# Casting later attention weights in two pairs of quarters and merging the scan's loads, in a one-core hybrid decoder layer

## The chip, the cores and the metric

The kernel runs on one core of a Trainium2 chip. A core has TensorE (PE: matrix products into PSUM), VectorE (DVE), ScalarE (ACT), GpSimd (POOL) and SyncE (SP), which here issues nearly all DMA transfers, from one queue, in order. Each engine works through its own instructions in order and waits where an instruction's operands or buffers are not ready. The metric is the device time of one execution in microseconds (us), lower is better; the time given for a kernel is a median of runs.

## The reference, cut to what matters

One layer with 1024 tokens and a model width of 1024, all in float32. Two groups of heads read the same normalised input.

```
proj = rms_norm(x, norm1_w) @ w_in          # q, k, v of attention; q, k, v, gate of DeltaNet
# group A: differential attention, 4 heads, two 64-wide softmax maps each
a    = softmax(q1 k1^T) - lam * softmax(q2 k2^T)      # causal
da_o = rms_norm(a @ v) * (1 - lam_init)
# group B: gated DeltaNet, 4 heads, in chunks, a scan that carries a state
v_new = u_c - w_c @ state
o     = (q_c * exp(g)) @ state + qk_c @ v_new
state = state * exp(g_last) + k_dec^T @ v_new
# both, then the MLP
x = x + concat(da_o, dn_o) @ w_out
x = x + relu(rms_norm(x, norm2_w) @ w_up)**2 @ w_down
```

## The kernel before

Every float32 product that must be exact is split: an operand is rounded to a short part (`wH`, `hH`: a cast on ACT) and a rest (`wL`, `hL`: a subtraction on DVE), and TensorE makes three products instead of one. So each piece of a weight passes through a DMA load into a raw buffer `wraw`, a cast on ACT (L200) and a subtraction on DVE (L201). There are two `wraw` buffers in the stage of interest, so a third load has to wait for the first buffer's cast and subtraction.

The stages follow each other roughly so: input norm and gates, DeltaNet projections (up to about 241 us of the profiled execution), then a long interleaved stage, then the MLP. In the interleaved stage run, side by side, as generators:

- `da_units`: the attention projections. There are six units, in the order k, q, v of heads 0 and 1, then k, q, v of heads 2 and 3. A unit has 256 columns of `w_in` (four quarters of 256 KB, each two of the eight k-blocks) and eight blocks of 128 rows; a block makes 24 products of 128x256 (L941 to L943). Behind each block ACT copies the result out of PSUM (L952 or L959 and L960). Blocks of q and k are normalised and turned: `da_turns` transposes them (L906, L907), ACT and DVE make `qa`, and SP stores it to `qk_d` (L912).
- `scan` and `scan_out`: the recurrence over eight chunks of 128 tokens. `load` (L788) brings four heads of `pka`, 192 KB each; the products at L796, L808 and L819 and their readers follow each other. `scan_out` loads `pkb` (L838, 128 KB a head, five buffers) and `zgt`, multiplies at L848 and L855 and stores `mixn_d`.
- `scores` and `values`: the attention itself by query tiles: loads of `qa` and `qb` (L1003, L1004), score products at L1061, L1062 and L1064, exponentials on ACT (L1070), transposes of the probabilities (L1097), their copy `at` on ACT (L1099), value products (L1109), and the copy `om` (L1114). Transposes and value products share two PSUM banks, `px0` and `px1`; a bank is free again once ACT, or ACT and DVE, have read it.
- `mix_loads`, `mixed` and `outproj`: the output projection, which has its weights from `load_unit` too. Its first half is called `pre` and is requested in the first block of the last unit.

Two things set the order of instructions. TensorE's order is written out by a planner, the class `Interleave`: each generator yields the time from which it may go on, `flow.chain` books estimated durations on ACT ("S"), DVE ("V") and POOL ("G"), and the ready generator with the lowest priority number is taken. `unit_time` books one unit's casts and subtractions and gives the due times `wt` of the four quarters. The order on ACT, DVE, POOL and SP is made by the framework's scheduler, which plays the instructions through with its own estimates; `tc.issue_after(x)` keeps an instruction from standing ahead of `x`.

In `load_unit` a quarter is loaded, cast and subtracted in one turn of a loop, and `da_units` calls it for unit i + 1 in the first block of unit i:

```
for k in range(0, nk, st):
    ...
    nc.sync.dma_start(raw[:, :, o:o + n], src[:, k0 + k:k0 + k + st, c0:c0 + n])
    ...
    S.copy(wh[:, k:k + st, :], raw)
    eng.tensor_tensor(wl[:, k:k + st, :], raw, wh[:, k:k + st, :].bitcast(F32), ALU.subtract)
```

Of the kernel before, what the change touches and what calls it, by code (L numbers as in the profile page):

```python
# [9 lines left out]
F32 = mybir.dt.float32  # L10
# [8 lines left out]
P = 128  # L19
SEQ = 1024  # L20
DM = 1024
KB = DM // P
NT = SEQ // P
HEADS = 4
# [97 lines left out]
def tile_hymba_layer(  # L122
# [6 lines left out]
    nc = tc.nc  # L129
    V, S, G, T = nc.vector, nc.scalar, nc.gpsimd, nc.tensor  # L130
# [3 lines left out]
    w_in_v = w_in[0].rearrange("(kb p) c -> p kb c", p=P)  # L134
# [48 lines left out]
    hH = hpool.tile([P, KB, SEQ], F32R, name="hH")  # L183
    hL = hpool.tile([P, KB, SEQ], F32R, name="hL")

    def load_unit(src, ranges, k0=0, nk=KB, eng=None, rp=None):
        eng = eng or V
        width = sum(n for _, n in ranges)
        wh, wl = staged("wH"), staged("wL")
        wh = wh[:, :nk * width].rearrange("p (k c) -> p k c", k=nk)  # L190
        wl = wl[:, :nk * width].rearrange("p (k c) -> p k c", k=nk)
        st = 2 * UC // width
        for k in range(0, nk, st):
            raw = rp.tile([P, 2 * UC], F32, tag="wraw", name="wraw", bufs=8) if rp else laid("wraw")
            raw = raw[:, :st * width].rearrange("p (k c) -> p k c", k=st)
            o = 0
            for c0, n in ranges:
                nc.sync.dma_start(raw[:, :, o:o + n], src[:, k0 + k:k0 + k + st, c0:c0 + n])
                o += n
            S.copy(wh[:, k:k + st, :], raw)  # L200
            eng.tensor_tensor(wl[:, k:k + st, :], raw, wh[:, k:k + st, :].bitcast(F32), ALU.subtract)  # L201
        return wh, wl

    def mm3(ps, lh, ll, rh, rl, n):
# [143 lines left out]
    with tc.manual_schedule(engines={T.engine, V.engine, S.engine}):  # L348
# [59 lines left out]
        for tb in range(2, NT):  # L408
            ps = z_mm(tb, 0)
# [11 lines left out]
            ps = z_mm(tb, 1)  # L421
# [351 lines left out]
    def unit_time(eng="V", rate=610.0):  # L773
        done = []
        for i in range(4):
            start = flow.now if i < 2 else done[i - 2]
            done.append(flow.chain(("S", 520.0), (eng, rate), start=start + DMA_T))
        return done

    def scan():  # L780
        St = {}
        psA = pA.tile([P, 512], F32, name="ps_A")
        PA = {h: psA[:, h * P:(h + 1) * P] for h in range(HEADS)}

        def load(c):
            pka = sb.tile([P, HEADS, 3, P], F32, tag="pka", name="pka", bufs=2)
            for h in range(HEADS):
                nc.sync.dma_start(pka[:, h], park_d[h, c, :, 0:3, :])  # L788
            return pka

        nxt = load(0)
        for c in range(NT):
            pk, rr_, yy = nxt, {}, {}
            if c > 0:
                for h in range(HEADS):
                    T.matmul(PA[h], pk[:, h, 0, :], St[h], start=True, stop=True)  # L796
                for h in range(HEADS):
                    i = cidx(h, c)
                    rr_[h] = sb.tile([P, P], F32, tag="sr", name="sr", bufs=4)
                    V.scalar_tensor_tensor(rr_[h], PA[h], neg_eg[:, i:i + 1], pk[:, h, 2, :], ALU.mult, ALU.add)  # L800
                flow.pe(4 * MM)
                yield flow.chain(*[vec(P, 60)] * 4), None
            else:
                for h in range(HEADS):
                    rr_[h] = pk[:, h, 2, :]
            for h in range(HEADS):
                Wc = W[h, c // 4][:, (c % 4) * P:(c % 4 + 1) * P]
                T.matmul(PA[h], Wc, rr_[h], start=True, stop=True)  # L808
            y4 = sb.tile([P, 512], F32, tag="sy", name="sy", bufs=2)
            S.copy(y4, psA)  # L810
            if c + 1 < NT:
                nxt = load(c + 1)
            flow.pe(4 * MM)
            yield flow.chain(act(512)), None
            Sold = dict(St)
            for h in range(HEADS):
                yy[h] = y4[:, h * P:(h + 1) * P]
                if c < NT - 1:
                    T.matmul(PA[h], pk[:, h, 1, :], yy[h], start=True, stop=True)  # L819
            if c < NT - 1:  # L820
                for h in range(HEADS):
                    i = cidx(h, c)
                    Sn = sb.tile([P, P], F32, tag=f"S{h}", name=f"S{h}", bufs=2)
                    if c > 0:
                        V.scalar_tensor_tensor(Sn, St[h], elast[:, i:i + 1], PA[h], ALU.mult, ALU.add)
                    else:
                        V.tensor_copy(Sn, PA[h])
                    St[h] = Sn
                flow.pe(4 * MM)
            flow.add(1, scan_out(c, Sold, yy), 0, "pB")  # L830
            if c < NT - 1:
                yield flow.chain(*[vec(P, 60)] * 4), None

    def scan_out(c, Sold, yy):
        pkb = {}
        for h in range(HEADS):
            pkb[h] = sb.tile([P, 2, P], F32, tag="pkb", name="pkb", bufs=5)
            nc.sync.dma_start(pkb[h], park_d[h, c, :, 3:5, :])  # L838
        zgt = sb.tile([P, 512], F32, tag="zgt", name="zgt", bufs=1)
        nc.sync.dma_start(zgt, zg_d[c])  # L840
        oc = sb.tile([P, 512], F32, tag="oc", name="oc", bufs=2)
        so = sb.tile([P, 4], F32, tag="so", name="so", bufs=2)
        osq = sb.tile([P, P], F32, tag="osq", name="osq", bufs=1)
        yield flow.now + 2500, "pB"
        if c > 0:
            o1 = pB.tile([P, 512], F32, tag="pB", name="ps_o1")
            for h in range(HEADS):
                T.matmul(o1[:, h * P:(h + 1) * P], pkb[h][:, 0, :], Sold[h], start=True, stop=True)  # L848
            V.tensor_tensor(v4(oc), v4(o1), bc_col(eg[:, c::8]), ALU.mult)
            flow.pe(4 * MM)  # L850
            flow.hold("pB", flow.chain(vec(512)))
            yield flow.now, "pB"
        o2 = pB.tile([P, 512], F32, tag="pB", name="ps_o2")
        for h in range(HEADS):
            T.matmul(o2[:, h * P:(h + 1) * P], pkb[h][:, 1, :], yy[h], start=True, stop=True)  # L855
        if c > 0:
            V.tensor_tensor(oc, oc, o2, ALU.add)
        else:
            S.copy(oc, o2)
        for h in range(HEADS):  # L860
            i = cidx(h, c)
            S.activation(osq, oc[:, h * P:(h + 1) * P], AF.Square, scale=rq[:, i:i + 1], accum_out=so[:, h:h + 1])
        f = sb.tile([P, 4], F32, tag="of", name="of", bufs=2)
        rstd(f, so, 1.0 / P, EPS, sb, "oft", 4)
        V.tensor_tensor(f, f, rq[:, c::8], ALU.mult)
        for h in range(HEADS):
            V.scalar_tensor_tensor(oc[:, h * P:(h + 1) * P], oc[:, h * P:(h + 1) * P], f[:, h:h + 1],
                                   zgt[:, h * P:(h + 1) * P], ALU.mult, ALU.mult)
        nc.sync.dma_start(mixn_d[c], oc)
        flow.pe(4 * MM)  # L870
        t = flow.chain(vec(512))
        flow.hold("pB", t)
        flow.chain(*[act(P, True)] * 4, vec(4), powr(4), vec(4), *[vec(P, 60)] * 4, start=t)
        if c == NT - 1:
            s2ctx.close()
            spctx.close()
            mp = ctx.enter_context(tc.tile_pool(name="mp", bufs=1, **left))
            pools["mp"] = mp
            for tb in tiles:
                accs[tb] = row_tile("acc")  # L880
            pools["a2"] = bctx.enter_context(tc.tile_pool(name="a2", bufs=1, **left))
            pools["be"] = bctx.enter_context(tc.tile_pool(name="be", bufs=2, **left))
            pools["rsc"] = scctx.enter_context(tc.tile_pool(name="rsc", bufs=1, space=PSUM, **right))
            state["scan"] = True
# [34 lines left out]
    def da_units():  # L919
        todo = [(g, kind) for g in range(2) for kind in (1, 0, 2)]  # L920

        def unit_w(i):
            g, kind = todo[i]
            return load_unit(w_in_v, [(512 * kind + 256 * g, 256)]), unit_time()

        w = unit_w(0)
        freed = [0.0, 0.0]
# [1 line left out]
        for i, (g, kind) in enumerate(todo):  # L929
            (wh, wl), wt = w  # L930
            for tb in range(NT):
# [17 lines left out]
                    yield flow.now + 50, None  # L949
                qn = sd.tile([P, 256], F32, tag="qn", name="qn", bufs=4)  # L950
                if kind == 2:
                    S.copy(qn, ps[:, :256])  # L952
                    st = nc.sync.dma_start(v_d[g, tb], qn.rearrange("p (h e) -> p h e", h=2))
                    if g == 1:
                        prefetch_x(st)
# [1 line left out]
                else:  # L957
                    sq = sd.tile([P, 256], F32, tag="qsq", name="qsq", bufs=1)
                    S.activation(sq, ps[:, :256], AF.Square)  # L959
                    S.copy(qn, ps[:, :256])  # L960
                    sn = sd.tile([P, 4], F32, tag="sn", name="sn", bufs=2)
                    V.tensor_reduce(sn, sq.rearrange("p (a d) -> p a d", d=DQK), axis=AX.X, op=ALU.add)
                    rn = sd.tile([P, 4], F32, tag="rn", name="rn", bufs=2)
# [4 lines left out]
                    freed[n % 2] = flow.chain(act(256), start=t - flow.HOP)  # L968
                    t = flow.chain(vec(256), vec(4), powr(4), vec(256), start=t - flow.HOP)
                    late.append((g, kind, tb, qn, t))  # L970
                n += 1
                state["units"] = n
            if kind == 2:
# [766 lines left out]
```

## Time and profile before

| what | value |
|---|---|
| median of 3 runs | 1268.11 us (1265.73 to 1270.84) |
| profiled execution | 1264.09 us, span in the profile 1262.1 us |
| granted TensorE clock | 0.999 |
| busy TensorE | 1234.1 us |
| busy DVE, ACT, POOL | 817.8, 614.0, 111.0 us |
| DMA | 200.02 MB, mean 158 GB/s |

In the rows, "out<-in" are tile names, "x" a count. A wait row names the engine and line that waited, what released it, and the total, the number and the longest wait in us. A timeline row has the start in us from the beginning of the span, the duration, engine, line and operation, and in brackets the idle time ahead of it with what ended it. "SPq" is the queue of DMA issues on SP. Products are pipelined: their durations overlap, and the distance of two starts tells how fast they follow each other.

### The profile page before, as it was taken

Reading aid. Unit: us, or ns where it says so; the run is one execution under the profiler, and the core shown is the slowest. Engines: PE = TensorE matmul, PEld = TensorE weight load, DVE = VectorE, ACT = ScalarE, POOL = GpSimd, SP = SyncE. Lnnn points to the kernel's source line nnn. Section 1 sums busy time; section 2 is a strip of 40 time slices with the busy share of each in tenths; the row PEclk is TensorE's granted clock in tenths of the full one; section 3 lists DMA queues with packets and bytes.
Section 4 is the critical chain, followed back from the end, with each engine's and each line's share of the span. In section 5 each row is a group of like instructions: output and inputs, shape, how many; then the busy total and the mean of one; then the engine's idle time right before and its main releaser. Section 6 shows DMA issues by size and latency. Waiting matters only on the chain.

```text
span 1262.1 us, 18992 instructions
## 1 busy us (share of the span) xinstructions
PE 1234.1 (98%) x6973; PEld 1061.5 (84%) x6973; DVE 817.8 (65%) x1416; ACT 614.0 (49%) x1237; POOL 111.0 (9%) x141
## 2 busy tenths in 40 slices
PE   8999999999999999998999999999999999999998
PEld 7988888899998998887887888888887788888887
DVE  6557797557657647776589555665566865687553
ACT  4469554334446545665557444554554333333331
POOL 2211110022212300011200000000000000000000
PEclk9999999999999999999999999999999999999999
DMA  6135554368858656334246534534368755433311
GB/s 240 39 94 144 142 165 118 82 191 260 258 144 245 168 179 162 99 91 143 94 147 207 191 136 167 183 134 144 124 226 323 302 200 200 167 101 100 128 39 67
DMA packets 165814, 200.02 MB, mean 158 GB/s; under 512 B 20905, under 2 KB 126169, under 8 KB 165722
## 3 DMA queue, kind: packets, MB, share of 16 engines
q1 hardware_dynamic: 165720, 198.82, 48.8%
q8 instruction: 55, 0.90, 0.3%
q14 instruction: 37, 0.30, 0.1%
q10 hardware_dynamic: 2, 0.00, 0.0%
HBM read 132.71 MB, written 66.06 MB: 157 GB/s over the span
## 4 chain that ended last, share of the span: by engine, by line
PE 85%; DMA 8%; DVE 3%; ACT 2%; issue 1%; SPq 1%; POOLq 0%; DVEq 0%; POOL 0%; ACTq 0%
PE X L1368 4%; PE X L1367 4%; PE X L1366 4%; PE ps_qk L941 4%; PE ps_qk L942 4%; PE ps_qk L943 4%; PE X L1662 3%; PE X L1663 3%; PE X L1661 3%; PE ps_dn L206 3%; PE ps_dn L207 3%; PE ps_dn L208 3%; PE Y L1366 2%; PE Y L1367 2%; PE Y L1368 2%; PE ps_o L1109 2%
## 5 line engine op out<-in xcount | busy, mean ns | idle before, releaser
L1285 ACT CAST hH<-ur 128x1024 fp32r<-128x1024 f32 x56 | 58.6, 1050 | 175.6 <-PE Z L1662 85.2
L1286 DVE TENSOR_TENSOR hL<-ur,hH 128x1024 fp32r<-128x1024 f32 x56 | 68.3, 1222 | 82.4 <-ACT hH L1285 82.3
L941 PE MATMUL ps_qk<-wH,hH 128*128 128x256 f32 x384 | 114.8, 299 | 0.1
L942 PE MATMUL ps_qk<-wL,hH 128*128 128x256 f32 x384 | 108.5, 283 | 0.0
L943 PE MATMUL ps_qk<-wH,hL 128*128 128x256 f32 x384 | 108.4, 282 | 0.0
L1286 DVE TENSOR_TENSOR op<-raw,op 128x1024 fp32r<-128x1024 f32 x48 | 58.7, 1223 | 74.2 <-PE X L1367 39.5
L1662 PE MATMUL X<-hL,hH 128*128 128x512 f32 x224 | 87.4, 390 | 2.7 <-DVE hL L1286 2.7
L1661 PE MATMUL X<-hH 128*128 128x512 f32 x224 | 87.5, 391 | 1.4 <-DVE b L1563 1.4
L1663 PE MATMUL X<-hH,hL 128*128 128x512 f32 x224 | 87.3, 390 | 0.0
L206 PE MATMUL ps_dn<-hH,wH 128*128 128x512 f32 x192 | 76.2, 397 | 0.3 <-ACT cp L561 0.3
L208 PE MATMUL ps_dn<-hH,wL 128*128 128x512 f32 x192 | 76.0, 396 | 0.0
L207 PE MATMUL ps_dn<-hL,wH 128*128 128x512 f32 x192 | 75.7, 395 | 0.0
L941 PEld LDWEIGHTS ps_qk<-wH,hH 128*128 128x128 f32 x384 | 73.5, 191 | 0.3 <-ACT qn L960 0.2
L942 PEld LDWEIGHTS ps_qk<-wL,hH 128*128 128x128 f32 x384 | 73.5, 191 | 0.0
L943 PEld LDWEIGHTS ps_qk<-wH,hL 128*128 128x128 f32 x384 | 73.2, 191 | 0.0
L1286 DVE TENSOR_TENSOR hL<-dw,hH 128x1024 fp32r<-128x1024 f32 x56 | 68.0, 1217 | 3.2 <-ACT hH L1285 3.2
L1285 ACT CAST op<-raw 128x1024 fp32r<-128x1024 f32 x48 | 50.4, 1052 | 36.9 <-PE Y L1368 19.9
L1285 ACT CAST hH<-dw 128x1024 fp32r<-128x1024 f32 x56 | 58.5, 1047 | 14.8 <-PE Z L1663 8.1
L565 DVE SCALAR_TENSOR_TENSOR cy<-cp,pv,cy 128x512 f32<-128x512 f32 x72 | 53.6, 745 | 13.1 <-ACT cy L563 12.4
L201 DVE TENSOR_TENSOR wL<-wraw,wH 128x512 fp32r<-128x512 f32 x64 | 43.8, 697 | 27.8 <-ACT wH L200 27.5
L200 ACT CAST wH<-wraw 128x512 fp32r<-128x512 f32 x64 | 38.2, 621 | 43.2 <-DMA wraw<-in_w_in_dram 28.5
L1070 ACT ACTIVATE pexp<-ps_sc,mx 128x128 f32<-128x128 f32 (+7 forms) x64 | 47.4, 741 | 22.9 <-DVE mx L1066 22.6
(354 smaller groups left out, 3459.8 us busy)
## 6 DMA issues: line engine op xcount, KB each, us to landing
ur<-ud SPq DMA_DIRECT2D x28, 1024.0 KB, 5.1
raw<-in_w_up_dram SPq DMA_DIRECT2D x32, 512.0 KB, 3.9
dw<-in_w_down_dram SPq DMA_DIRECT2D x32, 512.0 KB, 7.3
wraw<-in_w_in_dram SPq DMA_DIRECT2D x48, 256.0 KB, 2.9
qk_d<-qa SPq DMA_DIRECT2D x32, 256.0 KB, 3.6
ud<-ua SPq DMA_DIRECT2D x16, 512.0 KB, 2.6
ud<-s SPq DMA_DIRECT2D x16, 512.0 KB, 2.7
pka<-park_d SPq DMA_DIRECT2D x32, 192.0 KB, 3.8
```

The lines of the kernel that those rows point to most:

```text
L206: T.matmul(ps, lh(k), rh(k), start=(k == 0), stop=False)
L207: T.matmul(ps, lh(k), rl(k), start=False, stop=False)
L208: T.matmul(ps, ll(k), rh(k), start=False, stop=(k == n - 1))
L941: T.matmul(ps[:, :256], hH[:, k, sl], wh[:, k, :], start=(k == 0), stop=False)
L942: T.matmul(ps[:, :256], hH[:, k, sl], wl[:, k, :], start=False, stop=False)
L943: T.matmul(ps[:, :256], hL[:, k, sl], wh[:, k, :], start=False, stop=(k == KB - 1))
L1285: S.copy(dst[0], src)
L1286: V.tensor_tensor(dst[1], src, dst[0].bitcast(F32), ALU.subtract)
L1366: T.matmul(ps, op[0][:, k, cs], h[0][:, k, :], start=start and k == 0, stop=False, skip_group_check=True)
L1661: T.matmul(bank[t], v[0][:, j, sl], v[2][:, j], start=s0, stop=False, skip_group_check=True)
L1662: T.matmul(bank[t], v[0][:, j, sl], v[3][:, j], start=False, stop=False, skip_group_check=True)
L1663: T.matmul(bank[t], v[1][:, j, sl], v[2][:, j], start=False, stop=s1, skip_group_check=True)
```

## The change

`load_unit` gets a parameter `later`. With it, the two first quarters are loaded at once and everything else becomes a list of steps: split (cast and subtract) quarter 0, load quarter 2, split 1, load 3, split 2, split 3. Units 2 to 5 use it. In the unit before, behind the copy of block 3, four of these steps are issued, and behind the copy of block 6 the last two; each cast is kept behind that copy. For the planner, due times of these units become 0, and two pairs of cast and subtraction are booked at each of the two places. Units 0 and 1 and all other callers work as before.

The scan's four loads of `pka` for a chunk become one transfer of four heads. The four loads of `pkb` become two transfers of two heads, in three buffers of double size.

```
-    def load_unit(src, ranges, k0=0, nk=KB, eng=None, rp=None):
+    def load_unit(src, ranges, k0=0, nk=KB, eng=None, rp=None, later=None):
...
-        for k in range(0, nk, st):
+
+        def load(k):
             raw = rp.tile([P, 2 * UC], F32, tag="wraw", name="wraw", bufs=8) if rp else laid("wraw")
...
-            S.copy(wh[:, k:k + st, :], raw)
+            raws.append(raw)
+
+        def split_part(k, behind=None):
+            raw = raws.pop(0)
+            with tc.issue_after(behind.ins) if behind else ExitStack():
+                S.copy(wh[:, k:k + st, :], raw)
             eng.tensor_tensor(wl[:, k:k + st, :], raw, wh[:, k:k + st, :].bitcast(F32), ALU.subtract)
+
+        raws, ks = [], list(range(0, nk, st))
+        if later is None:
+            for k in ks:
+                load(k)
+                split_part(k)
+            return wh, wl
+        load(ks[0])
+        load(ks[1])
+        for i, k in enumerate(ks):
+            later.append(lambda behind, k=k: split_part(k, behind))
+            if i < 2:
+                later.append(lambda behind, k=ks[i + 2]: load(k))
         return wh, wl
...
             pka = sb.tile([P, HEADS, 3, P], F32, tag="pka", name="pka", bufs=2)
-            for h in range(HEADS):
-                nc.sync.dma_start(pka[:, h], park_d[h, c, :, 0:3, :])
+            nc.sync.dma_start(pka, park_d[:, c, :, 0:3, :].rearrange("h p s e -> p h s e"))
...
-        for h in range(HEADS):
-            pkb[h] = sb.tile([P, 2, P], F32, tag="pkb", name="pkb", bufs=5)
-            nc.sync.dma_start(pkb[h], park_d[h, c, :, 3:5, :])
+        for h in (0, 2):
+            t = sb.tile([P, 2, 2, P], F32, tag="pkb", name="pkb", bufs=3)
+            nc.sync.dma_start(t, park_d[h:h + 2, c, :, 3:5, :].rearrange("h p s e -> p h s e"))
+            pkb[h], pkb[h + 1] = t[:, 0], t[:, 1]
...
+        steps = []
+
         def unit_w(i):
             g, kind = todo[i]
-            return load_unit(w_in_v, [(512 * kind + 256 * g, 256)]), unit_time()
+            if i < 2:
+                return load_unit(w_in_v, [(512 * kind + 256 * g, 256)]), unit_time()
+            return load_unit(w_in_v, [(512 * kind + 256 * g, 256)], later=steps), [0.0] * 4
...
-                    S.copy(qn, ps[:, :256])
+                    act_at = S.copy(qn, ps[:, :256])
...
+                if steps and tb in (3, 6):
+
+                    for _ in range(4 if tb == 3 else 2):
+                        steps.pop(0)(act_at)
+                    for _ in range(2):
+                        flow.chain(("S", 520.0), ("V", 610.0))
                 n += 1
```

More of the change, by code (lines that the diff above doesn't have):

```diff
@@ L959, in da_units @@
                     S.activation(sq, ps[:, :256], AF.Square)
-                    S.copy(qn, ps[:, :256])
+                    act_at = S.copy(qn, ps[:, :256])
                     sn = sd.tile([P, 4], F32, tag="sn", name="sn", bufs=2)
```

## The prediction

> **What bounds the kernel now.** First the page: the span, the busy time of the engines, the share of the chain of work by engine, and the transfers that the edit touches.
>
> ```profile
> span 1262.1 us, 18992 instructions
> PE 1234.1 (98%) x6973; PEld 1061.5 (84%) x6973; DVE 817.8 (65%) x1416; ACT 614.0 (49%) x1237; POOL 111.0 (9%) x141
> ...
> PE 85%; DMA 8%; DVE 3%; ACT 2%; issue 1%; SPq 1%; POOLq 0%; DVEq 0%; POOL 0%; ACTq 0%
> ...
> ur<-ud SPq DMA_DIRECT2D x28, 1024.0 KB, 5.1
> ...
> dw<-in_w_down_dram SPq DMA_DIRECT2D x32, 512.0 KB, 7.3
> wraw<-in_w_in_dram SPq DMA_DIRECT2D x48, 256.0 KB, 2.9
> ...
> pka<-park_d SPq DMA_DIRECT2D x32, 192.0 KB, 3.8
> ```
>
> In the last rows stand the count, the size and the median us from issue to landing; two more rows of the same kind, from the full list of transfers:
>
> ```profile
> qa<-qk_d SPq DMA_DIRECT2D x66, 64.0 KB, 2.4
> ...
> acc<-acc_d SPq DMA_DIRECT2D x8, 512.0 KB, 11.9
> ```
>
> TensorE is busy for 98% of the span. Its work is the same in both programs (6583 instructions of the same kinds), so the edit can only move the remaining 28 us of gaps and the small cost of changing from one group of products to another. The next view says how much of that lies where the order changes. In the changed program's order TensorE's instructions differ only from about 285 us to about 447 us of this trace; before and behind it they stand in the same order, and so do ACT's. Two stretches by engine (columns: stretch and length, PE, PEld, DVE, ACT, POOL busy, clock, DMA share, GB/s), then TensorE's waits from 275 to 447 us (total, times, longest).
>
> ```profile
> 280.00:345.00 65.00, 64.92 (x559) 64.75 (x558) 44.68 (x139) 28.12 (x87) 16.44 (x16) 1.00 0.83 258
> 368.00:447.00 79.00, 75.30 (x615) 71.72 (x614) 51.82 (x145) 47.37 (x135) 22.48 (x24) 1.00 0.76 216
> ```
>
> ```profile
> PE ps_qkt L906 <- ACT at L1099: 2.7, 1, 2.7
> PE ps_sc L1061 <- ACT pexp L1070: 0.7, 1, 0.7
> PE ps_qkt L906 <- ACT om L1114: 0.2, 1, 0.2
> ```
>
> The scan's stretch has 0.1 us of idle TensorE in 65 us. The whole region has 3.6 us of waits, and 2.7 of these are a single one. That wait is followed back through TensorE, ACT and the queue of SP:
>
> ```profile
> 400.45 0.28 PE L943 MATMUL ps_qk<-wH,hL 128*128 128x256 f32 x1
> 403.43 0.33 PE L906 MATMUL ps_qkt<-ident,qn 128*128 128x128 f32 x1 [2.70 <-ACT at L1099]
> ```
>
> ```profile
> 402.59 0.62 ACT L200 CAST wH<-wraw 128x512 fp32r<-128x512 f32 x1 [3.17 <-DMA wraw<-in_w_in_dram]
> 403.12 0.26 ACT L1099 COPY at<-ps_at 128x128 f32<-128x128 f32 x1
> ```
>
> ```profile
> 398.08 0.38 SPq L198 DMA_DIRECT2D wraw<-in_w_in_dram  x1
> 398.56 0.58 SPq L1003 DMA_DIRECT2D qa<-qk_d  x1
> ```
>
> A quarter of the next unit's weights is issued at 398.08 and lands at 402.59, 4.5 us later. ACT has already come to the cast of that quarter and stands there for 3.17 us. The copy `at` behind it keeps a PSUM bank occupied, and the transposes at L906 need that bank. This is head-of-line blocking on ACT by a load issued too late.
>
> **The change part by part.**
>
> *Quarters of units 2 to 5 (16 casts, 16 subtractions, 16 loads).* Number and size stay. Quarters 0 and 1 are now cast behind block 3's copy, quarters 2 and 3 behind block 6's. Their loads are issued several blocks earlier (a block is 24 products of about 0.12 us, 2.9 us, against a landing of 2.9 to 4.5 us), so no cast of these units should meet a missing transfer: the 2.7 us go, and the 0.2 with them. The 0.7 stands behind an exponential of the scores, which stays: 0 for it. A gain of 2.9; at most 3.6, if that goes too, and at least 2.7. Is the weight still in time? In the changed order the shortest way from the end of block 6 to the product that needs quarter 2 is 4.3 us (unit 2), and to quarter 3, 5.0 us. Against it stand the copies, casts and a subtraction:
>
> ```profile
> 439.12 0.37 ACT L960 COPY qn<-ps_qk 128x256 f32<-128x256 f32 x1
> 439.38 1.15 ACT L200 CAST wH<-wraw 128x512 fp32r<-128x512 f32 x2
> ```
>
> ```profile
> 403.24 0.69 DVE L201 TENSOR_TENSOR wL<-wraw,wH 128x512 fp32r<-128x512 f32 x1 [3.21 <-ACT wH L200]
> ```
>
> 0.37 + 1.15 + 0.69 is 2.2 us, so 2 us of cover are left. If it were gone, TensorE would wait at the start of each of four units; I take 0.
>
> *Regrouping.* The planner no longer sees due times for these weights, and TensorE's order between 285 and 447 us has 11 groups fewer (934 instead of 945 runs of one output). A change of group costs one longer step, as the starts show:
>
> ```profile
> 439.39 0.36 PE L941 MATMUL ps_qk<-wH,hH 128*128 128x256 f32 x1
> 439.59 0.28 PE L942 MATMUL ps_qk<-wL,hH 128*128 128x256 f32 x1
> 439.70 0.28 PE L943 MATMUL ps_qk<-wH,hL 128*128 128x256 f32 x1
> ```
>
> 0.20 us instead of 0.12, so 11 x 0.08 = 0.9 us less; between 0, if other groups lose it, and 0.9.
>
> *The first half of the output weights (`pre`), not edited, but moved in effect.* Now its quarters 0 and 1 were loaded long ahead, because the two raw buffers were free after unit 5's early casts: issued at 404.66, cast at 439.38 without a wait. Quarters 2 and 3 do wait.
>
> ```profile
> 404.66 0.38 SPq L198 DMA_DIRECT2D wraw<-in_w_out_dram  x1
> ```
>
> ```profile
> 440.76 0.93 SPq L198 DMA_DIRECT2D wraw<-in_w_out_dram  x2
> ```
>
> ```profile
> 441.33 0.27 ACT L1114 COPY om<-ps_o 128x128 f32<-128x128 f32 x1 [0.63 <-PE ps_o L1109]
> ...
> 444.54 0.62 ACT L200 CAST wH<-wraw 128x512 fp32r<-128x512 f32 x1 [2.12 <-DMA wraw<-in_w_out_dram]
> ```
>
> Landing took 3.8 us there (440.76 to 444.54), and TensorE did not mind. In the changed program unit 5's last two quarters leave the raw buffers only behind block 6 of unit 4, while `pre` is still cast behind block 7: one block for the load. From the end of block 6: copies and casts 0.7 + 1.15, subtraction 0.69, so the load is issued at 2.6 and lands 2.9 to 3.8 us later, at 5.5 to 6.4; the second a little later; two casts end at 6.7 to 7.7. Behind them on ACT stands `om` (0.27), which frees the bank for the second of two transposes. By the changed order TensorE comes to it at 6.3: five groups of six products (3.6), score products 0.6, value products 1.8, transposes 0.3:
>
> ```profile
> 432.89 0.31 PE L1061 MATMUL ps_sc<-KS,qa 128*128 128x128 f32 x1
> ...
> 433.48 0.36 PE L941 MATMUL ps_qk<-wH,hH 128*128 128x256 f32 x1
> ...
> 435.00 1.95 PE L1109 MATMUL ps_o<-vt,at 128*128 128x128 f32 x16
> ...
> 436.78 0.27 PE L906 MATMUL ps_qkt<-ident,qn 128*128 128x128 f32 x1
> ```
>
> So it waits 0.7 to 1.7 us there; then quarters 2 and 3 are loaded behind these subtractions, and the copy `at` behind their casts is 0 to 1.4 us late for the next value products. Together 0.7 to 3.1; with the 4.5 us landing seen at 398.08 instead, 5. I take 1.9, the middle of the nearer rows.
>
> *Scan loads.* An issue of `pka` takes SP 0.42 us (the columns of the durations are least, median, most, in ns):
>
> ```profile
> L788 SPq DMA_DIRECT2D pka<-park_d x16: 319/422/486, 290.8 to 334.4; - x16
> ```
>
> With 40 issues fewer (24 of `pka`, 16 of `pkb`) SP is left some 16 us, but no wait of TensorE in this stretch ends on SP or on these loads: 0. The merged `pka` (768 KB) lands between 3.8 (192 KB) and 5.1 us (1024 KB); the gap from its free buffer to its use stays above 10 us: 0. The merged `pkb` (256 KB, three buffers) is tighter. The scan runs faster in the new order, and for chunks 5, 6 and 7 the products that read it come 5.6, 5.6 and 5.2 us behind those that free its buffer. Issue 0.4 plus today's landing in this stretch,
>
> ```profile
> DMA to landing us min/median/max: 4.7/4.8/4.8
> ```
>
> gives 5.2 and, with semaphores, some 5.4: a delay of about 0.5 us in all. It is 0 at the 2.9 us of `wraw`, and 6.7 us at the 7.3 us of `dw` (7.7 less 5.6, 5.6 and 5.2). I take 0.5, from the row of the same transfer.
>
> [...]
>
> *Query loads.* The scores of the fourth tile come 2.9 us earlier in the new order, 5.6 us behind those of the second, which free their `qa` and `qb`. SP needs four issues of 0.58, a store of `qk_d` and a load of `x` (some 0.4 each) between, 3.1 us, and the last lands 2.4 later: 5.5, just in time. The store itself waits for a transposed block, up to one group of products and its two copies, some 1.3 us: 0 to 1.3 late, I take 0.7, the middle, as no row is nearer to one end.
>
> Sum: -2.9 - 0.9 + 1.9 + 0.5 + 0.7 = -0.7 us. The profiled execution took 1264.09 us (span 1262.1 and 2.0 around it), so 1263.4 in a like execution. The median of the runs is 4.0 us above it, 1268.11; the median after should be 1267.4.
>
> **The rivals.**
>
> 1. *The gain stands alone.* `pre` lands in time, as quarters 2 and 3 at 440.76 hurt nobody now, and `pkb` and the queries land in time: -2.9 - 0.9 is -3.8, 1264.3. For it: 0.1 us idle in the scan. Against: `pre` has one block of 2.9 us for the 3.8 us of landing.
>
> 2. *`pre` takes the place of the late quarter.* The same blocking of ACT moves from unit 4 to unit 5. At 5 us the sum is +2.4, 1270.5: slower than before, within 0.5%. It decides where `pre` costs over 2.6 us, between the landings of 2.9 (0.7) and 3.8 (3.1): from about 3.6 us on. For it: the 3.8 us of the very load. Against: the median of 2.9.
>
> 3. *Late scan loads.* If merged `pkb` lands like `dw`, 6.7 in place of 0.5 makes the sum +5.5, 1273.6; at the 11.9 of `acc<-acc_d` each chunk is 6.7 to 7.1 us late and the sum is +19, 1287. TensorE then waits at L848 for two heads that came in one transfer. It costs over 0.5% from a landing of about 7.6 us on. For it: the DMA share of 0.83. Against: `pkb` in that load takes 4.8.
>
> 4. *Nothing.* The casts are written later, yet ACT's order in the changed program could put them where a wait costs as much: 1268.1. Against: in the changed order of SP each of these loads stands whole blocks ahead of its cast.
>
> **How the numbers follow.** About 0.5%, 6.3 us, is what a measurement of this kernel can tell from no change. My case, with rival 4 next to it, 0.55; rival 1 0.2; rival 2 0.14; rival 3 0.11. Only rival 3 passes 6.3 us above, and only in 0.08; nothing in the region can give 6.3 us below (3.6 + 0.9 is all), except a shift of the gaps outside it, 24 of the 28 us: 0.04. The runs spread from 1265.73 to 1270.84, so a median carries some 2 us. Range: 1264.3 less 2 to 1270.5 plus 2.5, that is 1262.3 to 1273; it leaves out the upper part of rival 3 and the ends of the spread, some 0.15.
>
> **What would show it.** Right: no cast of units 2 to 5 idle on `wraw<-in_w_in_dram`, the 2.70 row gone, and a new wait of one to three us near unit 5's first blocks that follows casts idle on `wraw<-in_w_out_dram`. `pka` x8 and `pkb` x16 issues. Wrong: waits of TensorE on L796, L848 or their ACT and DVE partners in the scan; waits at the start of units on `wL`; or longer gaps behind 447 us, where the order is the same and only arrival times move.

## The result: slower by 0.5%, and the profile after

The changed kernel takes 1273.09 us in the median of four runs (1273.0 to 1275.41) against 1267.83 us of four runs of the kernel before (1265.73 to 1270.84). The ratio is 1.0052, with a 95% interval of 1.0036 to 1.0068: slower by 0.52%. Run again beside other kernels (e5), the ratio was 1.0047 (1.0033 to 1.0061). The forecast was 1267.4 us, 0.7 under the kernel before, with a range of 1262.3 to 1273: the measured time is 5.7 us above the forecast, and the kernel became slower where a slight gain was expected.

The page of the changed kernel: span, busy time by engine, and the share of the chain of work by engine.

```profile
span 1271.3 us, 18939 instructions
PE 1237.5 (97%) x6973; PEld 1063.4 (84%) x6973; DVE 819.2 (64%) x1416; ACT 614.7 (48%) x1237; POOL 111.4 (9%) x141
...
PE 82%; DMA 9%; DVE 4%; ACT 2%; issue 1%; SPq 1%; POOL 1%; POOLq 0%; DVEq 0%; ACTq 0%
```

TensorE's instructions are the same in number and kind (6973 in both pages; the 6583 of the prediction stands in neither), and its busy time is up by 3.4 us: at a lower granted clock the same products take longer (those of 128x512 start 0.43 us apart at a clock of 0.50, from 1004.86 us on, and 0.23 us apart at 1.00, from 998.86 us on). The span is 9.2 us longer. By the starts of products 1.3 us of this arise before 130 us, where the programs are equal (the granted clock from 68.6 to 130 us was 0.97 in this execution and 1.00 in that of before). The stretch from the first product of the fifth attention block to that of the 45th of 48 has nearly all the rest: 269.19 to 452.92 before, 270.36 to 461.04 after, 6.9 us more. TensorE's waits of the changed kernel in that stretch (total, times, longest in us):

```profile
PE ps_sc L1091 <- DMA qa<-qk_d: 3.8, 1, 3.8
PE ps_qkt L926 <- ACT om L1144: 1.4, 1, 1.4
PE ps_o L868 <- DMA pkb<-park_d: 1.0, 1, 1.0
PE ps_sc L1091 <- ACT pexp L1100: 0.6, 1, 0.6
PE ps_qkt L926 <- DVE qn L990: 0.6, 1, 0.6
PE ps_sc L1092 <- DMA qb<-qk_d: 0.4, 1, 0.4
PE ps_qkt L926 <- ACT at L1129: 0.4, 1, 0.4
```

These are 8.2 us where the kernel before had 3.6 in the same stretch (the three rows that the prediction shows). The 2.7 us behind `at` are gone. The new large one is a wait of score products for the queries, `qa` and `qb`. In TensorE's order of time it is the third tile of head 0 (384 columns):

```profile
382.27 0.41 PE L1091 MATMUL ps_sc<-KS,qa 128*128 128x384 f32 x1 [3.78 <-DMA qa<-qk_d]
383.13 0.49 PE L1092 MATMUL ps_sc<-KS,qb 128*128 128x384 f32 x1 [0.44 <-DMA qb<-qk_d]
```

SP's queue says why the queries were late (start, duration of the issue, line, transfer):

```profile
367.56 1.26 SPq L1018 DMA_DIRECT2D KS<-qk_d  x2
369.66 0.38 SPq L1025 DMA_DIRECT2D vt<-v_d  x1
370.08 2.04 SPq L1018 DMA_DIRECT2D KS<-qk_d  x2
372.16 1.20 SPq L1025 DMA_DIRECT2D vt<-v_d  x1
373.41 2.42 SPq L1184 DMA_DIRECT2D mt<-mixn_d  x2
375.93 0.58 SPq L1033 DMA_DIRECT2D qa<-qk_d  x1
```

Ahead of the third tile's queries stand four loads of head 1's keys (`KS`, 256 KB each), two of values (`vt`, 512 KB each, one of head 0 and one of head 1) and two of `mt` (256 KB each): 2.5 MB, of which only head 0's values stood there before as well. In the kernel before the same queue had these queries first and the first of head 1's keys behind them:

```profile
369.74 0.60 SPq L1003 DMA_DIRECT2D qa<-qk_d  x1
...
371.69 0.61 SPq L1004 DMA_DIRECT2D qb<-qk_d  x1
372.40 0.53 SPq L198 DMA_DIRECT2D wraw<-in_w_in_dram  x1
372.97 1.26 SPq L988 DMA_DIRECT2D KS<-qk_d  x2
```

Nothing in the diff touches these loads. They wait for the scan's memory (`KS` and `vt` of head 1 and `mt` lie in it). In TensorE's new order the scan ends some 3 us earlier (its last store is issued at 364.35 against 367.46), and in SP's order, which the scheduler writes, they now stand ahead of the queries.

The wait costs more than itself. The stretches of the changed kernel around it (stretch and length, PE, PEld, DVE, ACT, POOL busy, clock, DMA share, GB/s):

```profile
378.50:382.27 3.77, 0.00 (x0) 0.03 (x1) 0.75 (x2) 0.00 (x0) 0.00 (x0) 1.00 1.07 313
382.27:383.13 0.86, 0.41 (x2) 0.19 (x2) 0.00 (x0) 0.00 (x0) 0.00 (x0) 1.00 1.04 343
383.13:386.00 2.87, 2.87 (x12) 2.43 (x13) 1.11 (x2) 1.47 (x5) 0.00 (x0) 0.53 0.88 257
386.00:388.00 2.00, 2.00 (x17) 2.00 (x16) 1.43 (x6) 1.50 (x7) 0.00 (x0) 0.82 0.53 127
```

Behind the pause the clock is 0.53 and then 0.82: 2.87 x 0.47 + 2.00 x 0.18 is 1.7 us of lost work. In the kernel before the pause of 2.70 us (400.73 to 403.43) had no such trail; the same view there, in two stretches of 3.41 us:

```profile
398.74:402.15 3.41, 1.99 (x17) 1.79 (x16) 1.29 (x3) 0.68 (x2) 0.38 (x1) 1.00 1.00 319
402.15:405.56 3.41, 2.13 (x18) 2.13 (x19) 2.10 (x6) 2.97 (x8) 0.00 (x0) 1.00 0.65 190
```

So the stretch adds up: 8.2 - 3.6 = 4.6 us of waits and 1.7 us of clock, 6.3 of the 6.9.

### The profile page after: what moved, and what is told of

Read it like the earlier page. It is cut to its first block, busy times and chain, and to the rows that moved or that the text cites. A ratio compares the mean times of both kernels' runs of the same rounds, so it can differ in the third digit from the quotient of the medians.

```text
span 1271.3 us, 18939 instructions
## 1 busy us (share of the span) xinstructions
PE 1237.5 (97%) x6973; PEld 1063.4 (84%) x6973; DVE 819.2 (64%) x1416; ACT 614.7 (48%) x1237; POOL 111.4 (9%) x141
## 4 chain that ended last, share of the span: by engine, by line
PE 82%; DMA 9%; DVE 4%; ACT 2%; issue 1%; SPq 1%; POOL 1%; POOLq 0%; DVEq 0%; ACTq 0%
PE X L1398 4%; PE X L1396 4%; PE X L1397 4%; PE X L1692 3%; PE X L1693 3%; PE X L1691 3%; PE ps_qk L965 3%; PE ps_dn L226 3%; PE ps_dn L228 3%; PE ps_dn L227 3%; PE ps_qk L967 3%; PE ps_qk L966 3%; PE Y L1396 2%; PE Y L1397 2%; PE Y L1398 2%; PE ps_o L1139 2%
## 5 line engine op out<-in xcount | busy, mean ns | idle before, releaser
L1096 DVE TENSOR_REDUCE mx<-ps_sc 128x1 f32<-128x128 f32 (+7 forms) x64 | 47.8, 754 | 25.0 <-PE ps_sc L1094 24.5
```

## The experiments

Three theories stood against each other for the loss. Q: the order of loads in SP's queue delays the queries, and the clock falls because of that wait. M: the merged transfers of the scan are slow and disturb what follows. C: the clock falls in these executions for another reason, and the wait is a small matter. Each kernel ran beside the kernel before on the same chip, in five rounds.

**e1_scan_only.** The kernel before with only the scan's loads merged.

```
+            nc.sync.dma_start(pka, park_d[:, c, :, 0:3, :].rearrange("h p s e -> p h s e"))
...
+        for h in (0, 2):
+            t = sb.tile([P, 2, 2, P], F32, tag="pkb", name="pkb", bufs=3)
```

> The kernel before with the scan loads merged alone; TensorE's order is that of before. Theory Q (the loss comes from the queue: the planner's new order ends the scan earlier, so keys and values of head 1 and the normalised mix, 2.5 MB, stand ahead of the third tile's queries): no change, within 2 us of before; the wait of 2.7 us behind the late quarter stays. Theory M (the merged transfers hold others up): slower by 3 us or more, with waits on pkb or in the scan. Theory C (the clock is granted lower whenever this kernel family runs longer, whatever the loads do): no statement on the mean, a clock of 0.996 or less.

Measured: 1263.37 us against 1265.35, ratio 0.9987 (0.9974 to 1.0). The merged loads alone cost nothing, and the median is even 2.0 us lower; M falls. Its wait in the stretch is the old one behind `at`, but it lasts 3.4 us in this execution, and behind it the clock falls (the wait ends at 404.48):

```profile
PE ps_qkt L906 <- ACT at L1099: 3.4, 1, 3.4
```

```profile
402.00:404.00 2.00, 0.00 (x0) 0.00 (x0) 0.00 (x0) 0.36 (x1) 0.00 (x0) 1.00 1.07 300
404.00:406.00 2.00, 1.52 (x7) 1.53 (x8) 1.49 (x5) 2.00 (x6) 0.00 (x0) 0.53 0.44 145
406.00:408.00 2.00, 2.00 (x13) 2.00 (x12) 2.00 (x4) 0.85 (x3) 0.00 (x0) 0.62 0.53 176
```

The same wait, at 2.70 us in the profile of the kernel before, left the clock alone. The last section comes back to this.

**e2_weights_only.** The changed kernel with the scan's loads as before, four and four.

```
-            nc.sync.dma_start(pka, park_d[:, c, :, 0:3, :].rearrange("h p s e -> p h s e"))
+            for h in range(HEADS):
+                nc.sync.dma_start(pka[:, h], park_d[h, c, :, 0:3, :])
...
```

> The changed kernel with the scan loads as before, four and four; TensorE's, ACT's and DVE's order are those of the changed kernel. Theory Q: nearly all of the loss, 4 to 5 us slower than before; a wait of 3 to 4 us on qa at the third tile's scores, and the clock dip behind it; the wait on pkb of 1.0 us gone. Theory M: back to the time of before, since no merged transfer is left. Theory C: slower by as much as the changed kernel, with or without the wait.

Measured: 1268.59 us against 1265.35, ratio 1.0028 (1.0014 to 1.0042). The loss comes with the weights' part: 3.2 us, where 4 to 5 were expected. Whether it is smaller than in the whole change the intervals don't say. The profile has the same wait, longer than the 3 to 4 us expected, and the clock after it:

```profile
PE ps_sc L1091 <- DMA qa<-qk_d: 6.1, 1, 6.1
```

```profile
380.00:384.00 4.00, 1.56 (x4) 1.02 (x5) 0.07 (x1) 0.00 (x0) 0.00 (x0) 0.50 0.58 170
384.00:388.00 4.00, 4.00 (x19) 3.69 (x19) 2.33 (x7) 2.83 (x9) 0.00 (x0) 0.50 0.61 198
```

**e3_queries_first.** The changed kernel, with head 1's loads and the first two of `mt` kept behind the fourth tile's last query load in SP's queue. TensorE's order is that of the changed kernel.

```
-                heads[1] = load_head(1, pools["a2"]), load_v(1, pools["a2"])
+                with tc.issue_after(asked[3].ins):
+                    heads[1] = load_head(1, pools["a2"]), load_v(1, pools["a2"])
...
-            nc.sync.dma_start(mt, (mixn_d if i < NT else mixa_d)[t])
+            with tc.issue_after(asked[3].ins) if i < 2 else ExitStack():
+                nc.sync.dma_start(mt, (mixn_d if i < NT else mixa_d)[t])
```

> The changed kernel with one thing moved: the loads of head 1's keys and values and the first two loads of the mix are kept behind the fourth tile's queries in SP's queue; TensorE's order is that of the changed kernel. Theory Q: the wait of 3.8 us on qa, the 1.4 us on qb (in part) and the dip of the clock to 0.66 behind them go; 5 to 6 us less than the changed kernel, so 1267 to 1268, near before; mean clock 0.998 or more apart from an early dip. Theory M: no change against the changed kernel. Theory C: clock stays at 0.993 to 0.996 and the time within 2 us of the changed kernel.

Measured: 1261.65 us against 1265.35, ratio 0.9975 (0.9961 to 0.9989). The order of a few loads on SP turns the loss into a gain, and the mean clock of the profile is 1.000, so C falls and Q holds. The gain is larger than expected: 9.6 us less than the changed kernel in e5, on the same chip, where 5 to 6 were forecast. Of the wait on `qa` 0.7 us is left, now at the fourth tile:

```profile
PE ps_qkt L926 <- ACT om L1148: 1.4, 1, 1.4
PE ps_o L868 <- DMA pkb<-park_d: 0.7, 1, 0.7
PE ps_sc L1095 <- DMA qa<-qk_d: 0.7, 1, 0.7
```

**e4_old_plan.** The changed kernel, but the planner sees units 2 to 5 as before (due times from `unit_time`, no bookings behind blocks 3 and 6), so that TensorE's order is that of the kernel before.

```
-            return load_unit(..., later=steps), [0.0] * 4
+            return load_unit(..., later=steps), unit_time()
...
-                    for _ in range(2):
-                        flow.chain(("S", 520.0), ("V", 610.0))
```

> The changed kernel, but the planner books units 2 to 5 as before (due times and bookings in the first block), which gives TensorE the order of before; loads, casts and merged transfers stay changed. Theory Q: the third tile's queries have 0.5 MB ahead of them instead of 2.5, no wait on qa there, and the 2.7 us behind the late quarter are gone: 1 to 3 us faster than before, if the first half of the output weights costs 1 to 2 us at unit 5. Theory M: slower than before by what e1 shows. Theory C: no statement on the mean, clock 0.996 or less.

Measured: 1262.74 us against 1265.35, ratio 0.997 (0.9957 to 0.9982). With the old order of TensorE, and with it the old end of the scan, the change as a whole brings 2.6 us, as expected. How much of this the later casts bring isn't shown: the merged loads alone (e1) gave 2.0 us, and the intervals overlap. No wait for queries of more than 0.4 us is left in the stretch, and the 2.70 us are gone, but other waits have come, two of them longer than 1 us:

```profile
PE ps_o L868 <- DMA pkb<-park_d: 1.6, 1, 1.6
PE ps_qkt L926 <- DVE rnt L251: 1.1, 1, 1.1
```

In this one execution the waits sum to 4.9 us against 3.6 in the profile of before, and the stretch from the fifth to the 45th block takes 186.5 us against 183.7, with 1.7 us lost to a clock of 0.50 from 325.24 to 328.65 us.

**e5_after_again.** The changed kernel once more, as the base of the next three.

> The changed kernel once more, beside the next three on one chip. Both theories: about 1.0 to 1.005 of the kernel before, with a wait of some 4 us of the third tile's first score products on qa. If it comes out no slower than the kernel before here, the loss is one of single executions and not of the order of the loads.

Measured: 1271.27 us against 1265.13, ratio 1.0047 (1.0033 to 1.0061). The wait on `qa` was 5.0 us here, with a clock of 0.50 behind it; `pkb` was not waited for.

**e7_only_x.** The changed kernel with only the two `mt` loads behind the queries.

```
+            with tc.issue_after(asked[3].ins) if i < 2 else ExitStack():
+                nc.sync.dma_start(mt, (mixn_d if i < NT else mixa_d)[t])
```

> The changed kernel with only the first two mt loads (0.5 MB, 2.4 us of SP's queue) put behind the queries; head 1's keys and values (1.5 MB) and head 0's values stay ahead of them. If what counts is the position in SP's queue, the queries are issued some 2.4 us earlier and the wait on qa shrinks from 3.8 to about 1.4 us, with a smaller loss of clock or none: about 1.000 of the kernel before. If the bytes in flight count (2 MB of 2.5 MB still ahead), the wait stays near 3 us and the ratio near 1.004.

Measured: 1268.38 us against 1265.13, ratio 1.0025 (1.0011 to 1.004), and the wait is 3.7 us: the expectation from the place in the queue (1.4 us) missed. The time lies between the two expectations, 2.9 us under e5, so `mt` may have a share that the overlapping intervals don't tell from zero. SP's queue and TensorE's row in this kernel:

```profile
369.32 3.20 SPq L1018 DMA_DIRECT2D KS<-qk_d  x2
372.56 1.27 SPq L1025 DMA_DIRECT2D vt<-v_d  x1
373.88 2.73 SPq L1033 DMA_DIRECT2D qa<-qk_d  x1
```

```profile
382.00 0.66 PE L1094 MATMUL ps_sc<-KS,qa 128*128 128x384 f32 x1 [3.69 <-DMA qa<-qk_d]
```

The first query load comes to its turn 2.05 us earlier than in the changed kernel (373.88 against 375.93), but its issue takes 2.73 us where 0.58 is usual. So the load of the tile's second half comes no earlier (377.32 against 377.24), and the products start at 382.00 instead of 382.27. What delays the queries is what still stands ahead of them, head 1's keys and values: they take SP's time and keep the DMA engines full. The 16 engines show it: their queue's packets took 100.1% of their time from 364 to 380 us here (packets, MB, share).

```profile
q1 hardware_dynamic: 5314, 3.18, 100.1%
```

**e8_only_heads.** The counterpart: only head 1's keys and values behind the queries, `mt` ahead of them.

```
+                with tc.issue_after(asked[3].ins):
+                    heads[1] = load_head(1, pools["a2"]), load_v(1, pools["a2"])
```

> The changed kernel with only head 1's keys and values (1.5 MB) put behind the queries; the two mt loads stay ahead. By the position in SP's queue the queries are issued some 5 us earlier: no wait on qa, no dip of the clock there, about 0.9975 of the kernel before, as with both moved. If the mt loads are the cause (they come last before the queries and took 2.42 us to issue), the wait stays over 2 us.

Measured: 1262.83 us against 1265.13, ratio 0.9981 (0.9968 to 0.9995). No wait for queries is left. The first query load has its turn at 369.95, and the six issued up to 380 us land in 2.9 us in the median; in the changed kernel the one issued at 377.24 took 4.94. The queue here, and the same 16 engines over the same 16 us:

```profile
364.64 0.91 SPq L1188 DMA_DIRECT2D mt<-mixn_d  x2
366.59 0.37 SPq L1025 DMA_DIRECT2D vt<-v_d  x1
369.95 0.58 SPq L1033 DMA_DIRECT2D qa<-qk_d  x1
```

```profile
q1 hardware_dynamic: 3885, 3.41, 70.3%
```

So it is head 1's keys and values, 1.5 MB, that make the wait. The bytes moved are about the same (3.41 and 3.18 MB), but with the keys in the stretch there are 5314 packets instead of 3885, and the engines are full.

**e6_pre_later** and, on another chip, **e11_pre_later_again.** e3's order of loads, and `pre` cast in two pairs as well, behind blocks 3 and 6 of unit 5. The planner's due times for `pre` go with it, so TensorE's order changes too, from about 440 us on. **e12_queries_first_again** is e3 once more, the base on that chip.

```
-                        pre.append((load_unit(w_out_v, [(0, 512)], 4, 4), unit_time()))
+                        pre.append((load_unit(w_out_v, [(0, 512)], 4, 4, later=steps), [0.0] * 4))
```

> The changed kernel with the first head-1 loads and the first two mt loads behind the queries (as in the run with the queries first), and the first half of the output weights (pre) also cast in two pairs, behind blocks 3 and 6 of unit 5. Theory that pre costs the wait on om at the start of unit 5 (1.4 us measured, 0.7 to 1.7 predicted): that wait goes, and the time is some 1 to 2 us under the run with the queries first, about 0.996 of the kernel before. Rival, that the wait is there because the last unit's transposes come earlier whatever pre does: it stays, 0.9975.

> The changed kernel with head 1's loads and the first two mt loads behind the queries, once more, as the base of the next three on the same chip: 0.9975 of the kernel before, as measured; waits on pkb of 0.7 and on om of 1.4 us.

> The same with pre cast in two pairs as well, once more. If pre costs the om wait of 1.4 us, this is 1 to 2 us under the base (0.999), with no om wait. If the 3 us seen between two chips were the chips, it is within 0.5 us of the base.

Measured: e6 1258.04 us against 1265.13, ratio 0.9952 (0.9935 to 0.9969); e12 1261.93 against 1266.97, 0.9964 (0.9951 to 0.9978); e11 1260.48 against the same, 0.9948 (0.9931 to 0.9964). e12 still has a wait of 1.2 us behind `om`, but in its profile not the 0.7 expected on `pkb`; e6 and e11 have no wait behind `om`. From the 41st to the 45th block TensorE takes 16.14 us in e12 and 14.56 in e11 for the same 121 products: `pre` cost 1.6 us. The medians agree (1.45), though their intervals overlap.

**e9_four_pkb** and **e10_both.** e12, and e11, with four loads of `pkb` in five buffers as before.

```
-        for h in (0, 2):
...
+        for h in range(HEADS):
+            pkb[h] = sb.tile([P, 2, P], F32, tag="pkb", name="pkb", bufs=5)
+            nc.sync.dma_start(pkb[h], park_d[h, c, :, 3:5, :])
```

> The base with four loads of pkb a chunk in five buffers, as in the kernel before; pka stays one transfer. If the merged pkb costs its wait (0.7 to 1.0 us at L868), this is 0.5 to 1 us under the base (0.9995) and shows no such wait. If four loads and SP's extra issues cost as much, it is the same or up to 1 us over.

> Both: pre cast in two pairs and four loads of pkb. If the two terms add up, about 2 us under the base, the fastest of the four.

Measured: e9 1261.24 us, ratio 0.9959 (0.9943 to 0.9974), 0.7 us under its base; e10 1257.89, 0.9939 (0.9918 to 0.9961), 2.6 under e11 and 4.0 under e12. Both lie within the intervals of their bases, so the price of the merged `pkb` is not told from zero by the times. e10 is the fastest of all: 0.6% faster than the kernel before. Its waits in the stretch:

```profile
PE ps_sc L1094 <- ACT wH L207: 1.1, 1, 1.1
PE ps_sc L1094 <- ACT pexp L1103: 0.6, 1, 0.6
PE ps_qkt L925 <- ACT at L1132: 0.4, 1, 0.4
```

## Why the prediction was wrong, step by step

- **Query loads (0.7 taken, 0 to 1.3): the step that failed.** It counted, ahead of the fourth tile's queries, four issues, a store and a load of `x`, and let the third tile be. What stood in the queue was 2.5 MB, 2 MB of it moved there by the scheduler, and it was the third tile that waited: 3.78 + 0.44 us, and 1.7 us of clock behind it, 5.9 in place of 0.7. For the clock the sum had no term at all. The changed order of SP's queue was there to be read before the run. The prediction followed the tiles that the diff names through it, but not the loads that it leaves alone. e3, e7 and e8 show the cause: head 1's keys and values ahead of the queries. With them behind, the wait is gone (e8); with `mt` alone behind, it stays (e7).
- **Quarters of units 2 to 5 (-2.9): the wait right, its worth in time not shown alone.** The 2.70 us are gone in every kernel with the later casts; in the changed order 0.4 us on `at` are left, and the 0.2 on `om` are gone. With TensorE's order held as before (e4) the median fell by 2.6 us, but the merged loads alone (e1) gave 2.0. No wait at the start of a unit on `wL` shows in the rows above, so the cover of 2 us held.
- **Regrouping (-0.9): not seen.** In e12, where the queue is repaired and the order is that of the changed kernel, the stretch from the fifth to the 45th block takes 183.03 us against 183.73 before. Its waits are 2.6 us against 3.6. So the rest became 0.3 longer, not 0.9 shorter. That term was 0 within what one profile shows.
- **`pre` (1.9 taken, 0.7 to 3.1): right in place, mechanism and size.** The chain on ACT and the wait of TensorE in the changed kernel:

```profile
445.39 0.62 ACT L207 CAST wH<-wraw 128x512 fp32r<-128x512 f32 x1 [1.63 <-DMA wraw<-in_w_out_dram]
446.29 0.62 ACT L207 CAST wH<-wraw 128x512 fp32r<-128x512 f32 x1 [0.29 <-DMA wraw<-in_w_out_dram]
446.82 0.26 ACT L1144 COPY om<-ps_o 128x128 f32<-128x128 f32 x1
```

```profile
447.13 0.33 PE L926 MATMUL ps_qkt<-ident,qn 128*128 128x128 f32 x1 [1.40 <-ACT om L1144]
```

Two casts idle on their loads, `om` behind them, 1.4 us lost; taken away in e11 it gave 1.6.

- **Merged `pkb` (0.5 taken, 0 to 6.7): the right size.** 1.0 us in the profile after, 1.1 in e8, 0.7 in e3, none in e5 and e12; 1.6 in e4, with TensorE's old order. The loads landed in 3.9 us in the median of the profile after, where 4.8 was taken. Rival 3, which gave 1273.6 for late scan loads, names nearly the measured time, but for the wrong reason: e1 has these loads and lost nothing.
- **Merged `pka` and SP's freed time (0): right.** No wait of TensorE on `pka`; e1 is no slower. The landing was longer than the 3.8 to 5.1 us given, 6.2 in the median of the profile after, but the gap of over 10 us covered it.

With the failed term at its measured size the sum is -0.7 + 5.2 = +4.5 us, and without the regrouping +5.4, where the medians differ by 5.3 (1273.09 less 1267.83). That it agrees so closely is partly luck: stretches with equal code differ by some 2 us between profiles (the clock from 948 to 1057 us is 0.98 in the profiles of before and after, 1.00 in those of e3, e5, e9 and e10).

One thing the prediction could not see in a single profile: the profiled execution of before, with a mean clock of 0.999, was one of the better ones. Over all its runs beside e1, e5 and e12 the mean granted clock was 0.9970, 0.9971 and 0.9968 (31, 28 and 17 runs), against 0.9990, 0.9986 and 0.9988 in the runs of e3, e8 and e12. A difference of 0.0015 to 0.0020 of some 1262 us is 1.9 to 2.5 us. With e12's 0.7 us in the stretch it makes about 3, and the medians gained 3.7, 2.3 and 5.0. One stretch of half clock more, of the kind that the last section describes, is 1.7 us. A likely cause is the old wait behind `at`: such a stretch followed it in e1's profile (3.42 us) and not in that of before (2.70 us). That one follows in most runs of the kernel before isn't shown, since the traces hold one execution of each kernel, and stays open.

## What to carry to other kernels

When a change lets one stage end earlier, list everything that waits for that stage's memory, and see where those transfers now stand in the queue, above all ahead of small loads that TensorE needs soon. Compare the whole order of the queue before and after, with bytes, not only the tiles that the diff names. In the changed order of TensorE a gain was left only with such loads tied behind the urgent ones: that one constraint was worth 8.4 us on one chip (e5 1271.27, e8 1262.83). And a pause of TensorE may cost more than its length: a further 1.7 us of clock behind the 3.78 us in the changed kernel, and none behind the 2.70 us in the kernel before.

## What the runs showed of the hardware that had not been expected

- A pause of TensorE can cost more than itself, and its length alone doesn't decide it. In the changed kernel's profile the clock is 0.50 for 3.41 us three times, from 82.94, 383.32 and 1004.54 us on. It is 0.50 for some 6.8 us beside the waits of 5.0 us in e5 and 3.7 in e7, and for some 10.2 us, to 388.6 us, at the 6.1 us of e2. With TensorE busy throughout, 3.41 us at a clock of 0.50 cost 1.7 us (an estimate, 3.41 x 0.5). The third of those in the changed kernel follows a pause of 2.18 us, shorter than the 2.70 us in the kernel before, which left the clock at 1.00:

```profile
1001.13:1004.54 3.41, 1.23 (x6) 0.72 (x5) 3.41 (x3) 2.59 (x3) 0.00 (x0) 1.00 1.04 410
1004.54:1007.95 3.41, 3.41 (x10) 2.65 (x9) 3.41 (x6) 0.45 (x1) 0.00 (x0) 0.50 1.02 407
```

TensorE was busy for 36% of the 3.41 us ahead of the half clock (1.23 us). In the two stretches of 3.41 us that hold the 2.70 us in the kernel before it was busy for 58% and 62% (1.99 and 2.13 us, shown with the result). So a pause of 2.18 us cost a further 1.7 us and one of 2.70 us nothing; what decides it is not shown.
- A load that has its turn in SP's queue may still wait. In e7, where the packets of the queue took 100.1% of the 16 engines' time from 364 to 380 us, the issue of one 64 KB load took 2.73 us, in e8, at 70.3%, 0.58. That of two `mt` loads took 2.42 us in the changed kernel, at 92.7%, and 0.91 in e8. Moving the queries ahead of `mt` alone (e7) started the products only 0.27 us earlier (382.00 against 382.27), in executions that stand within 0.2 us of each other at the 25th block; ahead of head 1's keys and values (e8) they left no wait.
